# Moving the overflow branch of a mixture of experts into its last first product, in a two-layer decoder trunk

## The chip, the cores and the metric

The kernel runs as one program on one core of a Trainium2 chip (trn2). The metric is the device time of one execution in microseconds. In the text TensorE is PE (PEld its weight loads), VectorE is DVE, ScalarE is ACT, GpSimd is POOL, and SP is the engine that issues most of the DMAs.

## What is computed

Two post-norm decoder layers over 256 positions of width 2048, all in float32. Layer 0 mixes with retention and a causal convolution, layer 1 (the odd one) with sparse attention. Behind each mixer stands the same grouped top-2 mixture of 16 experts of inner width 512, and a layer norm behind each half.

```python
def reference(x, ...):
    h = x
    for layer in range(DEPTH):                       # DEPTH = 2
        m = retention_conv_mixer(h, ...) if layer % 2 == 0 else dsa_mixer(h, ...)
        h = layer_norm(DEEPNORM_ALPHA * h + m, mix_ln_g[layer], mix_ln_b[layer])
        f = grouped_moe(h, router_w, router_b, moe_w_gu[layer], moe_w_down[layer])
        h = layer_norm(DEEPNORM_ALPHA * h + f, ffn_ln_g[layer], ffn_ln_b[layer])
    return h

def grouped_moe(x, router_w, router_b, w_gu, w_down):
    ...
    for e in range(N_EXPERTS):                       # 16
        a, b = jnp.split(xt @ w_gu[e], 2, axis=-1)
        y = y + gate[:, e:e + 1] * ((jax.nn.silu(a) * b) @ w_down[e])
    return y

# dsa_mixer begins with   proj = x @ w_in            # 2048 x 4176
```

## The kernel before

Weights stream from memory in chunks of 1 MB (`w0`, `w1`, ...) into a pool of 22 pages; `pump` issues the DMA of the next chunk on SP as soon as fewer than `ringmax` chunks are held, `take` hands the next one out and `done_chunk` frees it. Chunks 240 to 255 are those of layer 0's last pair of experts, 256 on those of the odd layer's input projection.

**The experts** (`moe`) run in eight pairs i, each in two halves j, one expert at a time. An expert takes up to 64 of the positions that chose it. `gather` picks their columns by one-hot products into `X[i]`, `gu(i, j)` is the first product (8 chunks, 32 float32 matmuls that write 64 rows each, L907), `turn` transposes the activated result (`sl`) into `gT`, and `down(i, j)` is the second product (L942). `weigh` scales its result by the gate and splits it into a rounded part `Yh` (ACT, L931) and the rest `Yl` (DVE, L932), both in the type fp32r. `scatter(i, t)` puts the pair's result back in place by one-hot products of `Yh` and `Yl` (L954) and adds it on DVE to the running sum `z` (L964), for t, the two halves of the positions. It runs behind the next pair's first product.

**The last pair** is cut otherwise. Behind `gu(7, 1)` and `turn` comes `overflow`: a branch (L1070) on the largest number of positions that an expert got. Only where that exceeds 64 does its body run, a general loop over all experts; on the inputs here it is skipped. Then `last_down` (from L975) does the last second product in four column blocks b of 512 columns, one chunk each (L1005), weighs each and places it: blocks 0 and 1 by `spread`, with the sum on DVE and its statistics by `bn_stats` (L993), blocks 2 and 3 by a product of the identity with the old sum `z` that opens the accumulation in a bank (`begin`, L983, tile `psb`), onto which the placed products fall, and ACT copies the bank back (L990). `begin(2)` runs right behind the branch, `begin(3)` behind block 1. `moments` turns the statistics into mean and scale (L674 to L676, the last step on POOL).

**The odd layer** starts with `norm` (L683 to L686), which applies that mean and scale to 512 columns, and `fold(kp)`, which transposes two blocks of 128 columns (`turned`, L712, tile `psz`) and writes them as `h32` (L717, L719). `parts(kp)` splits those into `hhi` (ACT) and `hlo` (DVE). `dense` then goes through units of two such blocks: `split` rounds a half chunk into `sp` (ACT, L234) and its rest (DVE or POOL, L237), and `mm` makes three fp32r products for each block and half of the positions, hhi by sp, hhi by the rest, hlo by sp (L266 to L268): 12 a unit. A group of 512 output columns is 8 units. The hooks `("pre", i)` stand ahead of unit i. The first two units are split early, in `last_down`, with POOL for the rest.

The order on each engine is that in which the code is written; each engine goes through its own list and waits on semaphores. At the end (`final`) DVE does 16 instructions of norm, gain and bias, and SP writes the result out.

## Time and profile before

| | us |
|---|---|
| runs | 1709.57, 1707.22, 1711.1 (median 1709.57) |
| the profiled execution | 1710.37 |
| its span, first to last instruction | 1708.6 |
| PE busy in the span | 1639.9 (96%) |
| DVE, ACT, POOL busy | 743.3, 499.5, 345.4 |

A row of a timeline has the start in us from the span's start, the busy time, the engine, the line, the operation, what it writes and reads, and in brackets how long the engine was idle and what released it. A float32 matmul leaves two records (two for each product, so x4 is two products of the code), an fp32r one leaves one. Busy times of PE overlap, since matmuls are pipelined: what one costs in a row of them is the distance from start to start.

### The profile page before, as it was taken

The page shows a single profiled execution, that of the slowest core. Times are in us where ns is not written, and L with a number is a line of the kernel's source. Part 1 is how long each engine was busy: PE and PEld are TensorE (multiplying, and loading weights), DVE is VectorE, ACT ScalarE, POOL GpSimd, SP SyncE. Part 2 cuts the span into 40 slices and gives each one's busy share as a digit, 9 for nine tenths or more (in the row PEclk, how much of TensorE's full clock was granted, in tenths as well). Part 3 has the DMA queues.
Part 4 walks back from the last instruction along what each step waited for, and adds up shares of the span by engine and source line. Part 5 has one row for each costly group of instructions (what it writes and reads, how often), then busy time and mean ns, then how long its engine had stood idle before and what let it go on. Part 6 is the DMA issues. An engine that isn't in the chain of part 4 may idle for free. (4 is left out here: it accounts for less than half of the span.)

```text
span 1708.6 us, 21350 instructions
## 1 busy us (share of the span) xinstructions
PE 1639.9 (96%) x8551; PEld 1039.2 (61%) x8551; DVE 743.3 (44%) x1348; ACT 499.5 (29%) x780; POOL 345.4 (20%) x218
## 2 busy tenths in 40 slices
PE   9999999999999999999789999999999999999984
PEld 7888887786454445444268788788644445454432
DVE  5699987533123222221264675664412212232225
ACT  5434345433111111111054535553311111111101
POOL 1446664540000000000024554444000000000010
PEclk9999999999999999999989999999999999999996
DMA  9655545858999999999954554357899999999992
GB/s 341 216 196 173 172 148 192 304 197 353 376 411 421 421 421 420 422 420 420 407 186 139 171 176 145 124 200 267 319 358 416 422 420 421 421 421 420 421 413 76
DMA packets 122860, 528.29 MB, mean 309 GB/s; under 512 B 10506, under 2 KB 10898, under 8 KB 74498
## 3 DMA queue, kind: packets, MB, share of 16 engines
q1 hardware_dynamic: 122130, 525.32, 79.1%
q8 instruction: 71, 1.16, 0.3%
q0 software_dynamic: 480, 1.46, 0.2%
q14 instruction: 35, 0.29, 0.0%
q10 hardware_dynamic: 144, 0.07, 0.0%
HBM read 524.71 MB, written 2.10 MB: 308 GB/s over the span
## 5 line engine op out<-in xcount | busy, mean ns | idle before, releaser
L907 PE MATMUL pgu<-w,X 128*64 128x512 f32 x2048 | 449.8, 594 | 7.3 <-DMA w<-in_moe_w_gu_dram 7.3
L237 POOL TENSOR_TENSOR sp<-w,sp 128x1024 fp32r<-128x1024 f32 (+1 forms) x108 | 272.9, 2535 | 398.9 <-ACT sp L234 383.4
L907 PEld LDWEIGHTS pgu<-w,X 128*64 128x64 f32 x2048 | 144.0, 137 | 295.2 <-issue 267.3
L234 ACT ACTIVATE sp<-w 128x1024 fp32r<-128x1024 f32 (+1 forms) x228 | 230.4, 1045 | 121.4 <-PE acc L268 64.1
L237 DVE TENSOR_TENSOR sp<-w,sp 128x1024 fp32r<-128x1024 f32 (+1 forms) x120 | 185.3, 1547 | 129.4 <-ACT sp L234 129.1
L932 DVE SCALAR_TENSOR_TENSOR Yl<-pdn,gs,Yh 64x512 fp32r<-64x512 f32 (+1 forms) x136 | 97.7, 718 | 272.2 <-ACT Yh L931 271.2
L942 PE MATMUL pdn<-w,gT 128*64 128x512 f32 x960 | 212.6, 595 | 0.9 <-ACT gT L919 0.9
L931 ACT ACTIVATE Yh<-pdn,gs 64x512 fp32r<-64x512 f32 (+1 forms) x136 | 89.4, 657 | 306.9 <-PE pdn L942 213.0
L911 DVE TENSOR_TENSOR sl<-sl,pgu 128x256 f32<-128x256 f32 x32 | 13.5, 422 | 352.1 <-ACT sl L910 352.1
L266 PE MATMUL acc<-sp,xhi 128*128 128x512 f32 x384 | 152.2, 396 | 0.0
L267 PE MATMUL acc<-sp,xhi 128*128 128x512 f32 x384 | 149.7, 390 | 0.3 <-DVE sp L237 0.3
L268 PE MATMUL acc<-sp,xlo 128*128 128x512 f32 x384 | 149.8, 390 | 0.0
L792 POOL COPY pt<-pt 128x128 f32<-128x128 f32 x16 | 5.1, 317 | 707.1 <-DVE pt L791 707.1
L942 PEld LDWEIGHTS pdn<-w,gT 128*64 128x64 f32 x960 | 66.3, 137 | 123.4 <-issue 117.1
L910 ACT ACTIVATE sl<-pgu 128x256 f32<-128x256 f32 x32 | 12.3, 385 | 385.2 <-PE pgu L907 385.2
L470 DVE SCALAR_TENSOR_TENSOR pcv<-up,cw,pcv 128x255 f32<-128x255 f32 (+14 forms) x240 | 113.2, 472 | 7.3
L266 PE MATMUL acc<-sp,hhi 128*128 128x512 f32 x256 | 106.0, 414 | 1.2 <-ACT hhi L1125 1.2
L268 PE MATMUL acc<-sp,hlo 128*128 128x512 f32 x256 | 101.0, 395 | 1.2 <-DVE hlo L1126 1.2
L267 PE MATMUL acc<-sp,hhi 128*128 128x512 f32 x256 | 100.5, 393 | 0.0
L267 PEld LDWEIGHTS acc<-sp,xhi 128*128 128x128 f32 x384 | 72.2, 188 | 15.4 <-DVE sp L237 1.0
L268 PEld LDWEIGHTS acc<-sp,xlo 128*128 128x128 f32 x384 | 72.1, 188 | 15.3
L266 PEld LDWEIGHTS acc<-sp,xhi 128*128 128x128 f32 x384 | 72.2, 188 | 14.8 <-ACT sp L234 0.4
(305 smaller groups left out, 2067.8 us busy)
## 6 DMA issues: line engine op xcount, KB each, us to landing
w<-in_moe_w_gu_dram SPq DMA_DIRECT2D x256, 1024.0 KB, 16.5
w<-in_moe_w_down_dram SPq DMA_DIRECT2D x128, 1024.0 KB, 19.5
w<-in_even_w_in_dram SPq DMA_DIRECT2D x46, 1024.0 KB, 5.5
w<-in_odd_w_in_dram SPq DMA_DIRECT2D x32, 1024.0 KB, 5.2
w<-in_even_w_out_dram SPq DMA_DIRECT2D x16, 1024.0 KB, 8.7
w<-in_odd_w_out_dram SPq DMA_DIRECT2D x16, 1024.0 KB, 5.3
acc<-in_x_dram SPq DMA_DIRECT2D x8, 256.0 KB, 8.3
w<-in_even_w_in_dram SPq DMA_DIRECT2D x4, 512.0 KB, 6.7
```

Of the source, the lines that this page charges most:

```text
L234: nc.scalar.activation(sp[:, 0], src, AF.Copy)
L237: eng.tensor_tensor(sp[:, 1], src, sp[:, 0].bitcast(F32), ALU.subtract)
L266: nc.tensor.matmul(ac, xh[:, x], wh, start=st, stop=False)
L267: nc.tensor.matmul(ac, xh[:, x], wl, start=False, stop=False)
L268: nc.tensor.matmul(ac, xl[:, x], wh, start=False, stop=en)
L470: nc.vector.scalar_tensor_tensor(y, up[:, c, 0:S - i], w, y, op0=ALU.mult, op1=ALU.add)
L907: nc.tensor.matmul(ps[h * 64:(h + 1) * 64, :], X[i][:, k, j * 64:(j + 1) * 64], wv[:, kk, :, h, :], start=k == 0, stop=k == KT - 1)
L910: nc.scalar.activation(sl, ps[:, 0:256], AF.Silu)
L911: V.tensor_tensor(sl, sl, ps[:, 256:512], ALU.mult)
L931: nc.scalar.activation(hi, po[r, :], AF.Copy, scale=g)
L932: V.scalar_tensor_tensor(lo, po[r, :], g, hi.bitcast(F32), op0=ALU.mult, op1=ALU.subtract)
L942: nc.tensor.matmul(po[b][half * 64:(half + 1) * 64, :], gT[:, c, h * 64:(h + 1) * 64], wv[:, half ^ j, 2 * b:2 * b + 2, :], start=kk == 0, ...
```

## The change

It does five things, the same for both layers where it concerns the experts.

1. The branch and its body move from behind `turn` into `gu(7, 1)`, ahead of its chunk 3 (w247). Between `turn` and `down(7, 0)` stands a new block with a `BRANCH_PREFETCH_HINT` that names the branch as likely taken, for PE alone, and one product of ones; every engine jumps into this block and out of it. The body's buffers change (four pages, one weight tile in place of two).
2. The old sums of blocks 2 and 3 (`begin`, moved out of `last_down`) come ahead of chunks 5 and 7 of `gu(7, 1)`, so behind the branch.
3. Columns 1024 to 2047 of the last pair are weighed whole, into a float32 tile `Yw`, half by ACT and half by DVE, and placed by one float32 product where two fp32r ones stood. Behind the last of them come 12 products of ones (`warm`).
4. The odd layer's first four units (w256, w257) take `h32` and the unsplit weights, one float32 product for each three. Their early splits are gone, `norm` and `fold` are spread over the hooks, and `parts(0)` to `parts(3)` come behind unit 4.
5. `scatter(i - 1, 0)` moves ahead of chunk 4 of `gu(i, 0)` and `scatter(i - 1, 1)` ahead of `turn`; `back` lays `h` out with the even columns of each 256 ahead of the odd ones, so `gather` reads it in a row and the first `scatter` reads it in two pieces; `ringmax` is 12 in place of 8 in the last pair until the branch.

```diff
-        if self.early and eng is None:
-            u["sp"] = self.early.popleft()["sp"]
-            return
...
+        if "x32" in u:
+            u["w32"] = i, t[:, u["sub"] * w:(u["sub"] + 1) * w, :]
+            return
...
+        if "x32" in u:
+
+            i, t32 = u["w32"]
+            for kk in range(w):
+                for t in ts:
+                    nc.tensor.matmul(g.acc[t], at(u["x32"], u["k"] + kk)[:, t * P:(t + 1) * P], t32[:, kk, :], start=u["first"] and kk == 0, stop=False)
+            if u["sub"] == u["nsub"] - 1:
+                self.done_chunk(i)
+            return
...
-            o = h[t][:, c * 512:(c + 1) * 512]
+            o = h[t][:, c * 512:(c + 1) * 512].rearrange("p (q r j) -> p q r j", q=2, r=2)
+            ps = ps.rearrange("p (q j r) -> p q r j", q=2, r=2)
...
+                k = c * 4 + b
+                for t in range(2):
+                    nc.tensor.matmul(ps[:, b * P:(b + 1) * P], h[t][:, k * P:(k + 1) * P], self.PT[i][:, t, 0:P], start=t == 0, stop=t == 1)
...
             for c in range(8):
+                if also and c in also:
+                    also[c]()
...
+        whole = lambda i, c0: i == 7 and c0 >= 512
...
+            if whole(i, c0):
+                y = Y["whole"][r, o, c0 - 512:c0 - 512 + n]
+                if half:
+                    nc.scalar.activation(y, po[r, :], AF.Copy, scale=g)
+                else:
+                    V.tensor_scalar(y, po[r, :], g, None, op0=ALU.mult)
+                return
...
+            one = whole(i, c * 256)
...
-                                     start=n == 0 and not begun, stop=n == 1, skip_group_check=begun)
+                at = GT[i][0][:, o, t * P:(t + 1) * P]
+                y = [Y[i][n][:, o, c * 256:(c + 1) * 256] for n in range(2)]
+                if one:
+                    at, y = at.bitcast(F32), [Y["whole"][:, o, c * 256 - 512:c * 256 - 256]]
+                for n in range(len(y)):
+                    nc.tensor.matmul(ps[:, o * 256:(o + 1) * 256], at, y[n], start=n == 0 and not begun, stop=n == len(y) - 1, skip_group_check=begun)
...
-                V.scalar_tensor_tensor(z, h[t][:, c * 512:(c + 1) * 512], ALPHA, ps, op0=ALU.mult, op1=ALU.add)
+                for q in range(2):
+                    s = slice(q * 256, (q + 1) * 256)
+                    v = lambda x: x[:, s].rearrange("p (j r) -> p j r", r=2)
+                    V.scalar_tensor_tensor(v(z), h[t][:, c * 512:(c + 1) * 512][:, s].rearrange("p (r j) -> p j r", r=2), ALPHA, v(ps),
+                                           op0=ALU.mult, op1=ALU.add)
...
+        def last_down(gT):
...
-            begin(2, self.bank)
...
-                for half in range(2):
+                for half in (1, 0):
                     weigh(7, 1, half, po, b * 256)
-                for u in early if b == 2 else ():
-                    self.split(u, nc.gpsimd)
-                    self.early.append(u)
                 if b:
                     finish(b - 1)
-                if b == 1:
-                    begin(3, self.psum)
             finish(3)
             self.drop(2)
+            self.warm(12)
...
             if i == 7:
-                self.ringmax = 8
+                self.ringmax = 12
             if 0 < i < 7:
                 self.onehot(i + 1)
 
 
-            sl = gu(i, 0)
             if i:
-                scatter(i - 1, 0)
+                sl = gu(i, 0, {4: lambda: scatter(i - 1, 0)})
+                scatter(i - 1, 1)
                 gT = turn(sl)
-                scatter(i - 1, 1)
             else:
+                sl = gu(i, 0)
                 self.onehot(1)
                 gates(0)
                 self.ringmax = 16
                 gT = turn(sl)
+            if i == 7:
+
+                with tc.block():
+                    tc.mark_branch_hint_location(f"general{layer}", hint="LikelyTaken", engines=[mybir.EngineType.PE])
+                    self.warm(1)
             down(i, 0, gT)
...
+
+            def general():
+                self.overflow(layer, rv, h, wide)
+                self.ringmax = 8
+                if before_last:
+                    before_last()
+            sl = gu(i, 1, {3: general, 5: lambda: begin(2, self.bank), 7: lambda: begin(3, self.psum)} if i == 7 else None)
...
-        gT = turn(sl)
-        self.overflow(layer, rv, h, wide)
-        if before_last:
-            before_last()
-        last_down(gT, self.units([Group(512, None, None)])[:2] if layer == 0 else ())
+        last_down(turn(sl))
...
-        hT = [wide("ohT", S) for i in range(2)]
+        hT = [self.page(f"ohT{i}", [P, 8, S]) for i in range(2)]
         gT = self.page("ogT", [P, 8, S])
-        ow = [self.page(f"ow{i}") for i in range(2)]
+        ow = self.page("ow")
...
         def fold(kp):
-            def f():
-                self.norms(kp)
-                self.turned(kp, h32[kp // 4][:, 2 * kp % 8:2 * kp % 8 + 2, :], 64, 96)
-            return f
+            return lambda: self.turned(kp, h32[kp // 4][:, 2 * kp % 8:2 * kp % 8 + 2, :], 64, 96)
+
+        def norm(c):
+            return lambda: self.norm(c)
 
         def parts(kp):
             def f():
@@ -1338,10 +1364,19 @@
         gout = [Group(512, lambda: (oo["hi"], oo["lo"]), self.z_done(c)) for c in range(4)]
         n = 4 + 8 * 8
         hooks = {("pre", n): [start_out], ("pre", n + 12): [last_heads, close_act]}
-        hooks["pre", 0] = [fold(0), fold(1), parts(0), fold(2), parts(1)]
-        for i in range(1, 7):
-            hooks["pre", i] = ([fold(i + 2)] if i + 2 < 8 else []) + [parts(i + 1)]
-        self.dense(self.units(gin) + self.units(gout, self.oorder), lambda: self.moe_begin(1), hooks)
+        us = self.units(gin)
+
+        for u in us[:4]:
+            u["x32"] = h32
+        hooks["pre", 0] = [norm(0), fold(0), fold(1), norm(1)]
+        hooks["pre", 1] = [fold(2)]
+        hooks["pre", 2] = [fold(3), norm(2)]
+        hooks["pre", 3] = [fold(4), parts(4)]
+        hooks["pre", 4] = [fold(5), parts(5), norm(3)]
+        hooks["pre", 5] = [fold(6), parts(6), parts(0)]
+        hooks["pre", 6] = [fold(7), parts(7), parts(1)]
+        hooks["pre", 7] = [parts(2), parts(3)]
+        self.dense(us + self.units(gout, self.oorder), lambda: self.moe_begin(1), hooks)
```

On PE at the end of layer 0's last pair, before: `pgu` is the first product's bank, `pst` the transposition, `psb` the old sums, `pdn` the last second product. The skipped body is left out.

```order
L907 MATMUL pgu_5398<-w251_5386,X_5136 64x512 x4
L917 MATMUL pst_5450<-cst_69,sl_5447 128x128 x2
L1070 COMPARE_AND_BRANCH
...
L983 MATMUL psb_5739<-z0_3557,cst_69 128x512
L983 MATMUL psb_5741<-z1_3558,cst_69 128x512
L1005 MATMUL pdn_5743<-w252_5403,gT_5453 64x256 x8
L1005 MATMUL pdn_5758<-w253_5409,gT_5453 64x256 x8
```

Now the announcement stands between the transposition of the half j = 0 and its second product (w240):

```order
L921 MATMUL pst_5373<-cst_69,sl_5346 128x128 x2
L1060 UNCONDITIONAL_BRANCH
L1433 BRANCH_PREFETCH_HINT
L365 LDWEIGHTS ones_75
L365 MATMUL warm_5380<-ones_75 128x512
L1060 UNCONDITIONAL_BRANCH
L955 MATMUL pdn_5382<-w240_5185,gT_5376 64x512 x2
```

and the branch itself ahead of w247, again with the body left out:

```order
L911 MATMUL pgu_5417<-w246_5265,X_5144 64x512 x4
L1095 COMPARE_AND_BRANCH
...
L911 MATMUL pgu_5417<-w247_5271,X_5144 64x512 x4
L911 MATMUL pgu_5417<-w248_5326,X_5144 64x512 x4
L1004 MATMUL psb_5735<-z0_3530,cst_69 128x512
L1004 MATMUL psb_5737<-z1_3531,cst_69 128x512
L911 MATMUL pgu_5417<-w249_5332,X_5144 64x512 x4
L911 MATMUL pgu_5417<-w250_5338,X_5144 64x512 x4
L1004 MATMUL psb_5747<-z0_3530,cst_69 128x512
L1004 MATMUL psb_5749<-z1_3531,cst_69 128x512
L911 MATMUL pgu_5417<-w251_5344,X_5144 64x512 x4
L921 MATMUL pst_5760<-cst_69,sl_5757 128x128 x2
L1027 MATMUL pdn_5765<-w252_5388,gT_5763 64x256 x8
```

The branch and both pairs of old sums now have first products behind them, and the four blocks of the last second product follow `turn` at once.

On DVE in `last_down`, blocks 0 to 3, before (two `Yl` a block, for the two halves of the rows):

```order
L964 TENSOR_TENSOR z1_3558<-psa_5780,z1_3558 128x512
L993 BN_STATS stats_102<-z1_3558 128x6
L932 SCALAR_TENSOR_TENSOR Yl7_5389<-pdn_5791,gs_5237,Yh7_5388 64x256 x2
L964 TENSOR_TENSOR z0_3557<-psa_5814,z0_3557 128x512
L993 BN_STATS stats_102<-z0_3557 128x6
L964 TENSOR_TENSOR z1_3558<-psa_5821,z1_3558 128x512
L993 BN_STATS stats_102<-z1_3558 128x6
L932 SCALAR_TENSOR_TENSOR Yl7_5389<-pdn_5828,gs_5237,Yh7_5388 64x256 x2
L991 BN_STATS stats_102<-psb_5739 128x6
L991 BN_STATS stats_102<-psb_5741 128x6
```

and now:

```order
L987 TENSOR_TENSOR z1_3531<-psa_5802,z1_3531 128x512
L1016 BN_STATS stats_102<-z1_3531 128x6
L941 TENSOR_SCALAR Yw_5410<-pdn_5809,gs_5245 64x256
L987 TENSOR_TENSOR z0_3530<-psa_5822,z0_3530 128x512
L1016 BN_STATS stats_102<-z0_3530 128x6
L987 TENSOR_TENSOR z1_3531<-psa_5829,z1_3531 128x512
L1016 BN_STATS stats_102<-z1_3531 128x6
L941 TENSOR_SCALAR Yw_5410<-pdn_5836,gs_5245 64x256
L1014 BN_STATS stats_102<-psb_5735 128x6
L1014 BN_STATS stats_102<-psb_5737 128x6
```

For blocks 2 and 3 one scaling stands where two subtractions stood.

On PE at the odd layer's first unit, before, from the last transposition ahead of it:

```order
L712 MATMUL psz_5911<-cst_69,z0_3557 128x128
L712 MATMUL psz_5911<-cst_69,z1_3558 128x128
L712 MATMUL psz_5911<-cst_69,z0_3557 128x128
L712 MATMUL psz_5911<-cst_69,z1_3558 128x128
L266 MATMUL acc_5926<-sp_5806,hhi0_5881 128x512
L267 MATMUL acc_5926<-sp_5806,hhi0_5881 128x512
L268 MATMUL acc_5926<-sp_5806,hlo0_5883 128x512
L266 MATMUL acc_5927<-sp_5806,hhi0_5881 128x512
L267 MATMUL acc_5927<-sp_5806,hhi0_5881 128x512
L268 MATMUL acc_5927<-sp_5806,hlo0_5883 128x512
```

and now the whole of that unit:

```order
L715 MATMUL psz_5907<-cst_69,z0_3530 128x128
L715 MATMUL psz_5907<-cst_69,z1_3531 128x128
L715 MATMUL psz_5907<-cst_69,z0_3530 128x128
L715 MATMUL psz_5907<-cst_69,z1_3531 128x128
L253 MATMUL acc_5916<-w256_5422,h320_5890 128x512
L253 MATMUL acc_5917<-w256_5422,h320_5890 128x512
L253 MATMUL acc_5916<-w256_5422,h320_5890 128x512
L253 MATMUL acc_5917<-w256_5422,h320_5890 128x512
```

Four float32 products with the weight chunk itself stand where twelve with its split parts stood.

## Rows read from the trace of the kernel before

**Rows 1.** windows by stretch: us, busy of each engine, granted clock, DMA share, GB/s
```profile
540.00:840.00 300.00, 297.25 (x1606) 139.96 (x1602) 72.33 (x126) 46.14 (x79) 1.30 (x4) 1.00 1.01 421
840.00:845.00 5.00, 2.61 (x12) 0.69 (x10) 0.42 (x1) 0.77 (x2) 0.00 (x0) 1.00 1.04 385
846.00:850.00 4.00, 0.00 (x0) 0.00 (x0) 0.00 (x0) 0.00 (x0) 0.00 (x0) 0.50 1.05 381
850.00:856.00 6.00, 5.68 (x14) 2.41 (x16) 0.00 (x0) 0.00 (x0) 0.00 (x0) 0.50 1.05 386
870.00:882.00 12.00, 7.26 (x25) 5.93 (x26) 7.57 (x17) 7.08 (x13) 2.23 (x3) 0.50 0.78 250
```

**Rows 2.** timeline of TensorE, layer 0's end: start, us, [idle before <- releaser]
```profile
798.79 14.01 PE L907 MATMUL pgu<-w,X 128*64 128x512 f32 x64
...
828.34 1.94 PE L907 MATMUL pgu<-w,X 128*64 128x512 f32 x8 [0.55 <-DMA w<-in_moe_w_gu_dram]
...
840.82 1.94 PE L907 MATMUL pgu<-w,X 128*64 128x512 f32 x8 [0.58 <-DMA w<-in_moe_w_gu_dram]
843.70 0.44 PE L917 MATMUL pst<-cst,sl 128*128 128x128 f32 x2 [0.94 <-DVE sl L911]
850.32 3.75 PE L983 MATMUL psb<-z,cst 128*128 128x512 f32 x4 [6.19 <-PEq L1070]
854.00 4.67 PE L1005 MATMUL pdn<-w,gT 128*64 128x256 f32 x32
...
859.99 1.88 PE L983 MATMUL psb<-z,cst 128*128 128x512 f32 x4
861.80 1.95 PE L1005 MATMUL pdn<-w,gT 128*64 128x256 f32 x16
...
869.50 0.41 PE L954 MATMUL psb<-Yh,gtt 128*128 128x256 f32 x1 [1.58 <-ACT Yh L931]
...
879.51 0.80 PE L266 MATMUL acc<-sp,hhi 128*128 128x512 f32 x1 [1.20 <-ACT hhi L1125]
```

**Rows 3.** TensorE's waits by releaser: total us, times, longest us
```profile
PE psb L983 <- PEq L1070: 12.1, 2, 6.2
PE pgu L907 <- DMA w<-in_moe_w_gu_dram: 7.3, 14, 0.7
PE psb L954 <- ACT Yh L931: 3.2, 2, 1.6
```

**Rows 4.** timelines of TensorE and VectorE over layer 1's end
```profile
1660.75 1.94 PE L907 MATMUL pgu<-w,X 128*64 128x512 f32 x8 [0.65 <-DMA w<-in_moe_w_gu_dram]
...
1669.99 3.75 PE L983 MATMUL psb<-z,cst 128*128 128x512 f32 x4 [5.92 <-PEq L1070]
...
1691.48 0.26 DVE L674 BATCH_NORM_AGGREGATE mv<-stats 128x2 f32<-128x24 f32 x1
```

**Rows 5.** the page of the profile: its span
```profile
span 1708.6 us, 21350 instructions
```

**Rows 6.** timelines of VectorE and GpSimd over the same end of layer 0
```profile
864.29 0.48 DVE L932 SCALAR_TENSOR_TENSOR Yl<-pdn,gs,Yh 64x256 fp32r<-64x256 f32 x1 [0.80 <-ACT Yh L931]
...
865.83 0.69 DVE L964 TENSOR_TENSOR z<-psa,z 128x512 f32<-128x512 f32 x1
866.56 0.69 DVE L993 BATCH_NORM_STATS2 stats<-z 128x6 f32<-128x512 f32 x1
...
868.48 0.46 DVE L932 SCALAR_TENSOR_TENSOR Yl<-pdn,gs,Yh 64x256 fp32r<-64x256 f32 x1
...
874.06 0.54 POOL L676 TENSOR_TENSOR rs<-mv,neghalf 128x1 f32<-128x1 f32 x1 [0.55 <-DVE mv L675]
```

**Rows 7.** timeline of TensorE in the odd layer's first units
```profile
893.76 0.60 PE L712 MATMUL psz<-cst,z 128*128 128x128 f32 x4
...
896.95 0.60 PE L712 MATMUL psz<-cst,z 128*128 128x128 f32 x4
...
904.96 0.50 PE L268 MATMUL acc<-sp,hlo 128*128 128x512 f32 x1 [0.93 <-DVE hlo L1126]
```

More of the change, by code (lines that the diff above doesn't have):

```diff
@@ L87, in __init__ @@
         self.tasks = deque()
-        self.early = deque()
         self.credit = 0
@@ L235, in split @@
         self.nsplit += 1
-        eng = eng or (nc.gpsimd if self.nsplit % 2 == 0 and self.pool_split else nc.vector)
+        eng = nc.gpsimd if self.nsplit % 2 == 0 and self.pool_split else nc.vector
         eng.tensor_tensor(sp[:, 1], src, sp[:, 0].bitcast(F32), ALU.subtract)
@@ L698, in normed @@
                 nc.vector.tensor_scalar(z, z, m, rs, op0=ALU.subtract, op1=ALU.mult)
-    def norms(self, kp):
-        for c in ((0, 1), (2,), (3,))[kp] if kp < 3 else ():
-            self.norm(c)
     def turned(self, kp, out, gc, bc):
@@ L945, in down @@
                 Y[i] = [self.page(f"Y{n}{i}", [P, 2, 1024], F32R) for n in "hl"]
+                if i == 7:
+                    Y["whole"] = wide("Yw", 512)
             for b in range(2):
@@ L973, in scatter, with begin @@
                 self.drop(2)
-        def last_down(gT, early):
-            begun = {}
-            def begin(b, alloc):
-                for t in range(2):
-                    ps = begun[b, t] = alloc("psb")
-                    nc.tensor.matmul(ps, self.ident, self.acc[t][:, b * 512:(b + 1) * 512], start=True, stop=False, skip_group_check=True)
+        begun = {}
+        def begin(b, alloc):
+            for t in range(2):
+                ps = begun[b, t] = alloc("psb")
+                nc.tensor.matmul(ps, self.ident, self.acc[t][:, b * 512:(b + 1) * 512], start=True, stop=False, skip_group_check=True)
+        def last_down(gT):
             def finish(b):
```

30 lines of the change are left out of this document (13 added, 17 removed).

## The prediction

> **What bounds the kernel now.** I read the windows first, by stage. From 540 to 840 us the DMA engines are busy throughout and move 421 GB/s [rows 1]: the experts' chunks of 1 MB come every 2.49 us, whatever the engines do. TensorE is busy in 297 of these 300 us, but its busy time says little: a chunk of the first product takes 1.75 us where chunks lie ready (64 records in 14.01 us, eight a chunk), and at the end of the layer each chunk has a wait of 0.55 us ahead of it [rows 2]. So in the experts' stage the stream of weights is the bound, and moves inside it are free as long as TensorE is back in step when the last chunk of the first product lands, at 840.8 us in layer 0.
>
> What follows that landing is a bare chain, and there the time is to be had. The waits by releaser put 12.1 us on TensorE's own sequencer at the branch, in two pieces, one a layer; nothing else of TensorE's comes near, the 14 waits for expert chunks together are 7.3 [rows 3]. The timelines show it in place: the transposition ends at 844.14, then 6.19 us without anything until 850.32, and 5.92 in layer 1 [rows 2, 4]. The clock adds to that. It falls to 0.50 of 2.4 GHz (1.2 GHz) in the idle stretch and stays there until 856, and again from 870 to 882, behind a last wait of 1.58 us and the norm [rows 1, 2]. At 1.2 GHz the two old sums of block 2 take 3.7 us; the same pair at full clock, block 3's, takes 1.81 from start to start [rows 2].
>
> **The sum for layer 0,** from the profiled execution (span 1708.6 [rows 5], time 1710.37).
>
> *Branch and old sums.* The branch now comes ahead of w247, so behind w246, which is done at 830.3 [rows 2]. If the announcement works, TensorE goes on with w247 at 830.83 when it lands. From there, with 1.75 us a chunk, landings 2.49 apart and 1.81 for a pair of old sums: w247 to 832.6, w248 from 833.3 to 835.1, old sums to 836.9, w249 to 838.6, w250 to 840.4, old sums to 842.2, w251 to 844.0. Before, it was done at 842.76. So 3.6 us of old sums and the branch cost 1.2 us there, the rest lies beside the stream. Two of those sums stood in the bare chain at half clock (3.7 us), two more at full clock (1.8).
>
> *The second product.* Before, from the end of the first product to the end of blocks 0 and 1 it is 842.76 to 858.67, 15.9 us: 1.9 for activation and transposition, the branch, the old sums, and 4.67 for the two blocks, in part at half clock [rows 2]. Now it is 1.9 and twice 1.87: 5.6 us, with TensorE never idle for longer than the activation, so I take full clock. Blocks 0 and 1 end at 849.6, 9.1 us sooner. A transfer could take the place of the wait: the last four chunks come at 385 GB/s [rows 1], 2.72 us each, so they land at 843.5, 846.3, 849.0 and 851.7, and they are wanted at 845.9, 847.8, 850.8 and 854. Hidden, by 1.5 us at least.
>
> *Weighing and placing.* Now VectorE is late next. Behind block 1 it does the last two `Yl` (end 851.7, each after ACT's half), then sum and statistics of both halves for block 0 and for block 1 (8 instructions of 0.69), two scalings of at most 0.46 in place of four `Yl`, four statistics with some 0.7 of waiting for ACT's copies, and the moments, 0.54 of them on POOL [rows 6]. That ends at about 862.4; from blocks 0 and 1 12.8 us, where before it was 15.9 (858.67 to 874.60). Before, the old sums of block 3 lay in it, the early splits on ACT, and a `Yl` that stood in line until 868.48 [rows 6] and held TensorE for the 1.58 us (3.2 over both layers [rows 3]). The whole columns cost TensorE no more: a float32 product of 256 columns is half of the 0.9 of an old sum, two fp32r ones take 0.24, so four of them are 1.8 us for 0.95, beside VectorE's chain. Mean and scale are ready 12.2 us sooner.
>
> *The odd layer.* From there to the first product it was 4.9 us (879.51 [rows 2]), with norm of 1024 columns and the split of `h` in it and the transpositions at half clock. Now one norm, four transpositions and two writes stand in it: between 2.0 (first write only is waited for) and 2.7; I take 2.4, a gain of 2.5, since the 12 products of ones reach to about 862 and leave short gaps. Units 0 to 3 took 14.6 us from 879.51 to the first product of unit 4 at 894.1, the first of them at half clock. Now each is four float32 products of 0.9, no row of this shape being there but the old sum's, plus 0.36 of transpositions (893.76 to 894.12 in a unit of 3.19 [rows 7]): 15.9, a loss of 1.3. At half clock for the first two it would be 3 more. The splits put off to units 5 to 7 can hold TensorE as `hlo` did before (0.93 [rows 7]), or no longer: between 1 us lost and 1 gained, taken as nothing. Layer 0 gains 12.2 + 2.5 - 1.3 = 13.4.
>
> **Layer 1** has the same chain to its first aggregation: 1662.69 to 1691.48 [rows 4]. In layer 0's new order that point falls 17.6 us behind the old end of the first product (860.4 against 842.76), so at 1680.3: 11.2 sooner. The norm and the writes behind it stay.
>
> **What costs nothing.** The moved `scatter`, the other layout of `h` and its 16 half-size sums on VectorE lie under the stream (VectorE busy 72 of 300 us [rows 1]); were the stream not the bound, they would cost some 2 us in all. The jumps into and out of the announcing block are the unknown: no row shows an unconditional jump in mid-program. Their targets are the next instructions, so nothing should have to be fetched; the other end is a stall like the branch's. On SP, VectorE, ACT and POOL even that would be covered, SP having eight chunks under way and the others some 15 us until the activation. [...]
>
> The sum: 13.4 + 11.2 = 24.6 off 1710.37 is 1685.8; the profiled execution is 0.8 above the median of the runs, so **1685**. Its own range is 1679 to 1691, by the half clock, the units 5 to 7 and some 2 us of error in VectorE's chain.
>
> **Rival 1: the announcement does nothing.** Then the stall of 5.9 to 6.2 us comes behind w246, TensorE resumes at 836.5, and five chunks and four old sums make 12.4 us: 848.9, which is 4.9 later than above, and 3 more if the clock falls as it did before, with 6 us at 0.50 behind the stall [rows 1]. Twice that is 10 to 16: 1695 to 1701, **1697**. For it speaks that the stream can't cover a stall so near to its end; against it, that 12 us and some hundred instructions lie between announcement and branch, twice the stall. [...]
>
> **Rival 2: the jumps stall TensorE, and it ends slower.** If each of the two jumps on TensorE is itself a fetch of 6 us at the announcement, and the branch too, 18.3 us of stall and 3.6 of old sums meet 3.7 us of slack a layer (half of 7.3 [rows 3]): 18 us late, where the forecast has 1.2. That is 34 over both layers, **1719**, more with the clock. It decides from 12 us a layer, where the gain is used up. Against it: the targets are adjacent.
>
> **Rival 3: VectorE or the odd layer's start holds most of the gain back,** with the clock at 1.2 GHz through units 0 and 1 (3 us), `hlo` late (2 us) and block copies late in both layers (2 us): **1692**. For it speaks that VectorE has no slack behind block 1; against it, that its instructions there are counted and shown.
>
> **How the numbers follow.** Forecast 0.65, rival 1 0.22, rival 3 0.08, rival 2 0.03, and 0.02 for no change. A measurement of this kernel tells 0.2% (3.4 us) from nothing. The range takes in the forecast's own and rivals 1 and 3: 1679 to 1701. Faster 0.95, same 0.02, slower 0.03.
>
> **What would show it.** Right: no wait of TensorE on its sequencer over 1 us near the branch, w251's product done within 2 us of its landing plus 1.75, no granted clock of 0.50 between 844 and 862, the first product of the odd layer 14 to 15 us sooner, layer 1's first aggregation 11 sooner against the same landing. Rival 1: a 6 us wait ahead of w247. Rival 2: one ahead of w240. Wrong in another way: a later landing of the last chunk, which would say that the stream was not the bound.

## The result, and the profile after

The changed kernel takes 1686.68 us (median of 4 runs, 1684.45 to 1687.28); the kernel before, on the same chip, 1710.34 (1707.22 to 1712.38). The ratio is 0.9861, 95% interval 0.9843 to 0.9879. The forecast was 1685, by a sum of 24.6 us; the profiled execution of the changed kernel has a span of 1685.5 us for 1708.6 [rows 5], 23.1 less.

TensorE's waits by releaser (total us, times, longest us), which answer to [rows 3]:

```profile
PE pdn L955 <- ACT gT L923: 8.0, 16, 0.5
...
PE pgu L911 <- DMA w<-in_moe_w_gu_dram: 0.9, 2, 0.5
...
PE pgu L911 <- PEq L1095: 0.3, 2, 0.2
```

The 12.1 us at the branch are 0.3. The waits for expert chunks fell from 7.3 to 0.9, and in their place stand 16 waits of 0.5 for the activation that copies `gT`: `scatter(i - 1, 1)`, now ahead of `turn`, no longer covers that copy. Both lie under the stream, so one replaces the other.

The timeline of TensorE at layer 0's end, to be laid beside [rows 2]:

```profile
827.03 5.32 PE L911 MATMUL pgu<-w,X 128*64 128x512 f32 x24
832.51 1.94 PE L911 MATMUL pgu<-w,X 128*64 128x512 f32 x8 [0.16 <-PEq L1095]
834.98 1.94 PE L911 MATMUL pgu<-w,X 128*64 128x512 f32 x8 [0.53 <-DMA w<-in_moe_w_gu_dram]
836.85 1.98 PE L1004 MATMUL psb<-z,cst 128*128 128x512 f32 x4
838.76 3.65 PE L911 MATMUL pgu<-w,X 128*64 128x512 f32 x16
842.34 1.98 PE L1004 MATMUL psb<-z,cst 128*128 128x512 f32 x4
844.26 1.94 PE L911 MATMUL pgu<-w,X 128*64 128x512 f32 x8
847.13 0.44 PE L921 MATMUL pst<-cst,sl 128*128 128x128 f32 x2 [0.94 <-DVE sl L915]
848.10 3.67 PE L1027 MATMUL pdn<-w,gT 128*64 128x256 f32 x32 [0.53 <-ACT gT L923]
...
855.80 0.39 PE L974 MATMUL psa<-Yh,gtt 128*128 128x256 f32 x1 [0.24 <-DVE z L987]
...
856.47 1.95 PE L1027 MATMUL pdn<-w,gT 128*64 128x256 f32 x16
858.35 3.72 PE L974 MATMUL psb<-Yw,gtt 128*128 128x256 f32 x16
861.90 2.75 PE L365 MATMUL warm<-ones 128*128 128x512 bf16 x12
865.63 1.28 PE L715 MATMUL psz<-cst,z 128*128 128x128 f32 x8 [0.97 <-DVE z L693]
867.11 3.70 PE L253 MATMUL acc<-w,h 128*128 128x512 f32 x8 [0.20 <-DVE h L722]
...
882.62 0.48 PE L274 MATMUL acc<-sp,hhi 128*128 128x512 f32 x1
```

Row by row: the branch costs 0.16 us ahead of w247 (832.51), where it cost 6.19. The old sums (L1004) stand between the chunks. Nothing then keeps TensorE waiting longer than the 0.94 and 0.53 us around the transposition, until the placed blocks end at 862; `warm` covers part of the norm, and the odd layer's first product starts at 867.11, 12.4 us sooner than before. The first product of unit 4 is at 882.62, for 894.12. The granted clock, the column ahead of the DMA share, which showed 0.50 in two stretches here [rows 1], is 1.00 from 840 to 870; the last two windows (us, busy time of PE, PEld, DVE, ACT and POOL, clock, DMA share, GB/s):

```profile
860.00:865.00 5.00, 4.66 (x22) 2.66 (x20) 3.67 (x10) 1.90 (x4) 1.08 (x2) 1.00 0.45 128
865.00:870.00 5.00, 4.17 (x15) 2.32 (x16) 1.94 (x5) 2.53 (x4) 0.00 (x0) 1.00 1.05 397
```

In layer 1 the scale is done on POOL at 1670.8, 23.4 us sooner than before, and TensorE's timeline shows the same at the branch:

```profile
1638.23 1.94 PE L911 MATMUL pgu<-w,X 128*64 128x512 f32 x8 [0.16 <-PEq L1095]
```

Two executions of the changed kernel stand in different places, though. In the one above w248 lands late enough to start at 834.98, before the change at 833.32. In a second execution of the same kernel (the row *changed, again* below) it starts at 833.49, and the span is 1684.0, 24.6 less than before. So I compare kernels below by distances from w248's start, which leave the stream's lateness out:

| kernel | w248 starts, layer 0 | to the mean and scale | from there to unit 4 | layer 1: the same chunk to the last scale | time, median | ratio to before |
|---|---|---|---|---|---|---|
| before | 833.32 | 41.31 | 19.49 | 40.29 | 1710.34 | 1 |
| changed | 834.98 | 29.89 | 17.75 | 29.31 | 1686.68 | 0.9861 |
| changed, again | 833.49 | 29.90 | 17.75 | 29.31 | 1686.43 | 0.9853 |
| e1, no announcement | (stall) | | 17.76 | | 1696.58 | 0.9921 |
| e6, announced one chunk ahead | (stall) | | 17.76 | | 1696.14 | 0.9910 |
| e10, announced three chunks ahead | 833.86 | 29.89 | 17.76 | 29.33 | 1687.82 | 0.9871 |
| e2, before with the announcement alone | 833.49 | 32.08 | 19.26 | 31.67 | 1692.19 | 0.9899 |
| e3, branch and sums late | 835.92 | 31.37 | 17.75 | 30.80 | 1690.55 | 0.9884 |
| e7, split last columns | 835.21 | 31.41 | 17.76 | 30.94 | 1691.69 | 0.9890 |
| e8, no products of ones | 835.90 | 29.90 | 20.11 | 29.33 | 1690.58 | 0.9874 |
| e11, early splits | 833.35 | 29.84 | 19.23 | 29.31 | 1688.13 | 0.9876 |
| e4, units split late | 835.41 | 29.89 | 25.09 | 29.31 | 1693.70 | 0.9894 |
| e5, part 5 undone | 836.36 | 29.90 | 17.76 | 29.32 | 1688.15 | 0.9862 |
| e9, sums in the idle spots | 836.41 | 27.75 | 17.76 | 27.18 | 1684.15 | 0.9846 |

Start times of rows of the timelines: w248's first product, VectorE's row that makes the negative mean by scale (in layer 1 POOL's last row of the scale), the first product of unit 4. Where nothing in the chain differs the distances agree within 0.06 us, while the times move by 2 us, and the ratios have intervals of plus and minus 0.0015 to 0.002 (2.5 to 3.5 us). A difference between two changed kernels below 3 us is therefore read from the distances, not from the times. Where a row has (stall), w248 follows the stall without a wait, and its start is no measure of the stream.

### The profile page after: what moved, and what is told of

It reads as the page before. It is cut to its first block, busy times and chain, and to the rows that moved or that the text cites. A ratio compares the mean times of both kernels' runs of the same rounds, so it can differ in the third digit from the quotient of the medians.

```text
span 1685.5 us, 21370 instructions
## 1 busy us (share of the span) xinstructions
PE 1636.4 (97%) x8561; PEld 1029.7 (61%) x8561; DVE 739.5 (44%) x1357; ACT 493.4 (29%) x770; POOL 339.3 (20%) x215
## 3 DMA queue, kind: packets, MB, share of 16 engines
q0 software_dynamic: 480, 1.46, 0.2%
## 5 line engine op out<-in xcount | busy, mean ns | idle before, releaser
L236 POOL TENSOR_TENSOR sp<-w,sp 128x1024 fp32r<-128x1024 f32 (+1 forms) x105 | 265.6, 2537 | 282.0 <-ACT sp L233 256.4
L233 ACT ACTIVATE sp<-w 128x1024 fp32r<-128x1024 f32 (+1 forms) x224 | 226.4, 1045 | 120.4 <-PE acc L276 64.0
L945 DVE SCALAR_TENSOR_TENSOR Yl<-pdn,gs,Yh 64x512 fp32r<-64x512 f32 (+1 forms) x124 | 90.8, 733 | 257.0 <-ACT Yh L944 249.3
L944 ACT ACTIVATE Yh<-pdn,gs 64x512 fp32r<-64x512 f32 (+1 forms) x124 | 82.9, 669 | 249.6 <-PE pdn L955 184.0
L274 PE MATMUL acc<-sp,hhi 128*128 128x512 f32 x240 | 98.7, 411 | 0.4 <-ACT hhi L1151 0.4
L276 PE MATMUL acc<-sp,hlo 128*128 128x512 f32 x240 | 94.0, 392 | 0.0
L275 PE MATMUL acc<-sp,hhi 128*128 128x512 f32 x240 | 93.6, 390 | 0.0
```

Of the source, the lines that this page charges most:

```text
L233: nc.scalar.activation(sp[:, 0], src, AF.Copy)
L236: eng.tensor_tensor(sp[:, 1], src, sp[:, 0].bitcast(F32), ALU.subtract)
L274: nc.tensor.matmul(ac, xh[:, x], wh, start=st, stop=False)
L275: nc.tensor.matmul(ac, xh[:, x], wl, start=False, stop=False)
L276: nc.tensor.matmul(ac, xl[:, x], wh, start=False, stop=en)
L944: nc.scalar.activation(hi, po[r, :], AF.Copy, scale=g)
```

## The experiments

**The announcement, taken away (e1) and alone (e2).** e1 is the changed kernel without the block; e2 the kernel before with it.

```diff
-            if i == 7:
-                with tc.block():
-                    tc.mark_branch_hint_location(f"general{layer}", hint="LikelyTaken", engines=[mybir.EngineType.PE])
-                    self.warm(1)
             down(i, 0, gT)
```

> The changed kernel without the announcing block (no hint, no product of ones in it, no jumps); all else as in the changed kernel. Theory (the announcement does the work): TensorE stands on its sequencer for 5.9 to 6.2 us ahead of w247 in each layer, as it did at the branch before. Since TensorE is just in step with the stream there (it waited 0.53 us for w248), nearly all of it comes out behind w251: 5.5 us a layer, 11 in all, and up to 3 more a layer if the clock falls to 1.2 GHz in the stall: 1698 to 1704 us. Rival (the place alone hides the branch, the announcement is idle): no wait over 1 us ahead of w247, 1685 to 1688 us.

> The kernel before with the announcing block alone, between turn and down of expert 7,0; the branch stays behind the last transposition. Theory (the announcement alone takes the stall away wherever the branch stands): the 12.1 us on TensorE's sequencer fall below 1, the clock stays at 2.4 GHz, so layer 0's blocks 0 and 1 end near 850.5 instead of 858.67, 8 us sooner, and layer 1 gains as much: 1692 to 1696 us. Rival (a branch is cheap only under the stream): 1708 to 1712 us.

TensorE's timelines around the branch, in e1 in each layer, then in e2:

```profile
825.68 5.32 PE L911 MATMUL pgu<-w,X 128*64 128x512 f32 x24
835.12 5.35 PE L911 MATMUL pgu<-w,X 128*64 128x512 f32 x16 [4.12 <-PEq L1090]
840.40 1.99 PE L1004 MATMUL psb<-z,cst 128*128 128x512 f32 x4
```

```profile
1645.04 5.35 PE L911 MATMUL pgu<-w,X 128*64 128x512 f32 x16 [3.40 <-PEq L1090]
```

```profile
843.84 0.44 PE L917 MATMUL pst<-cst,sl 128*128 128x128 f32 x2 [0.94 <-DVE sl L911]
844.42 1.95 PE L983 MATMUL psb<-z,cst 128*128 128x512 f32 x4
```

Without the announcement the stall is back, ahead of w247, and the time rises to 1696.6 (1692.2 to 1700.6), ratio 0.9921 [0.9902, 0.9941]. It is the announcement, then, that takes the stall away, and not the place. The stall is smaller than the theory had it: 4.12 and 3.40 us, not 5.9 to 6.2, and the time lies under the theory's 1698 to 1704. The clock falls as well, for a shorter time than the theory allowed. Windows of e1 behind the stall in each layer (the granted clock ahead of the DMA share):

```profile
837.00:839.00 2.00, 2.00 (x7) 0.61 (x4) 0.00 (x0) 0.00 (x0) 0.00 (x0) 0.50 1.00 398
1646.00:1648.00 2.00, 2.00 (x6) 0.60 (x4) 0.00 (x0) 0.00 (x0) 2.00 (x2) 0.50 0.99 409
```

At 0.50, w247 and w248 take 5.28 us in each layer (835.12 to 840.40 in layer 0), where two chunks at full clock take 3.58 (838.76 to 842.34 in the changed kernel): 1.7 us a layer, not 3. Stalls and clock are 10.9 us in both layers together. Not all of it comes out, since waits for chunks fall away: from w244's start to the mean and scale it is 42.74 us in e1 and 37.84 and 37.98 in the two executions of the changed kernel, in layer 1, to the last scale, 41.44 for 37.07 and 37.05. So 9.2 to 9.3 us come out; the profiled span is 7.9 to 9.4 us longer than the two of the changed kernel.

e2 shows the other side: with the branch where it always was, the block alone takes the stall from 6.19 to less than 0.2 us and the time to 1692.2, 18.1 us less than before, of the change's 24. By the distances it is 9.23 and 0.23 in layer 0 and 8.62 in layer 1, 18.1 together. The stalls themselves are 11.8 of that; most of the rest is clock, for behind the stall two old sums take 3.68 us from start to start (850.32 to 854.00 [rows 2]), and in e2 1.89.

The two sides do not add up. All parts without the announcement (e1) bring 13.7 us, the announcement alone 18.1, both together 24: in part they save the same time. Which part of the block does it, the hint or the jumps around it, neither run tells; a block without the hint was not tried.

**How early it must be announced (e6, e10).** The block moves to one chunk and to three chunks ahead of the branch.

```diff
-gu(i, 1, {3: general, ...
+gu(i, 1, {2: announce, 3: general, ...      # e6
+gu(i, 1, {0: announce, 3: general, ...      # e10
```

> The changed kernel with the announcing block moved to one chunk ahead of the branch, ahead of w246, so that some 2 us lie between them and not 12. Theory (the announcement starts a load that takes about 6 us from then on): a stall of 3.5 to 4.2 us remains ahead of w247 in each layer, 1693 to 1697 us. Rival A (it works at once): no stall, 1685 to 1688 us. Rival B (it needs the whole of the old distance): about 6 us, as without it, 1698 to 1704 us.

> The changed kernel with the announcing block ahead of w244, three chunks (5.3 us of products) ahead of the branch, where it was one chunk with no effect and four chunks of down and three of gu with full effect. Theory (the announcement starts a load of some 6 us, and TensorE's sequencer reads it ahead of the array): most of the stall is gone, under 1.5 us a layer, 1686 to 1689 us. Rival (it takes nearly the old distance): 3.4 to 4.1 us a layer remain, 1693 to 1698 us.

The product of ones in the block (`warm`, L365) and the first row behind the branch, in e6 and in e10:

```profile
830.40 0.39 PE L365 MATMUL warm<-ones 128*128 128x512 bf16 x1
...
836.53 5.35 PE L911 MATMUL pgu<-w,X 128*64 128x512 f32 x16 [3.87 <-PEq L1095]
```

```profile
825.82 0.39 PE L365 MATMUL warm<-ones 128*128 128x512 bf16 x1
...
831.67 1.94 PE L911 MATMUL pgu<-w,X 128*64 128x512 f32 x8 [0.16 <-PEq L1095]
```

One chunk ahead the announcement gives nothing: 3.87 and 3.61 us, 7.5 together as in e1. Three chunks ahead it gives all: 0.16. The numbers of my theory for e6 came in (a stall of 3.5 to 4.2 us, and 1696.1 us in 1693 to 1697), but not as the theory meant them: it took them for the rest of a stall of 6 us, and without any announcement the stall is no more than 4.1. Rival B, about 6 us, fell. One reading fits these rows: from the block's product to the first product behind the branch it is 6.13 us in e6 (830.40 to 836.53; 5.86 in layer 1), the 5.9 to 6.2 of the stall before; in e10 5.85 us lie between them, with 0.16 of it a wait, and in the changed kernel 13. So it looks as if a load of some 6 us started when TensorE gets to the block, and in e1 as if it started some 2 us before TensorE gets to the branch. That is an argument from four rows; the last section has what bears on it. A block two chunks ahead, which should leave some 2 us, was not tried.

**The place of the branch and the old sums (e3).** Announced as in the changed kernel, but branch and sums behind the transposition.

```diff
-            sl = gu(i, 1, {3: general, 5: ..., 7: ...} if i == 7 else None)
+            sl = gu(i, 1)
...
-        last_down(turn(sl))
+        gT = turn(sl)
+        general()
+        begin(2, self.bank)
+        begin(3, self.psum)
+        last_down(gT)
```

> The changed kernel with the branch and the four old sums of each layer back behind the last transposition; the announcement stays where it is. Theory (announced, the branch costs 0.2 us anywhere, and the place matters for the 3.7 us of old sums alone): w251 is done about 1.8 us sooner, at its landing plus 1.9, and the four sums and the branch stand bare behind the transposition for 3.9 us: 2.1 us a layer lost, 1689 to 1693 us. Rival (the place under the stream hides the branch): a stall of about 6 us in each layer, 1698 us or more.

TensorE's timeline from w251 to the first second product:

```profile
843.45 1.94 PE L911 MATMUL pgu<-w,X 128*64 128x512 f32 x8 [0.61 <-DMA w<-in_moe_w_gu_dram]
846.91 3.67 PE L1004 MATMUL psb<-z,cst 128*128 128x512 f32 x8
850.51 2.81 PE L1027 MATMUL pdn<-w,gT 128*64 128x256 f32 x24
```

As the theory has it: no stall, w251 starts at its landing, and 3.6 us of old sums stand bare ahead of `pdn`. The loss is 1.48 and 1.49 us by the distances (2.1 expected: 3.2 us more between w251 and `pdn`, less the 1.75 by which w251 is earlier). Taken out of the changed kernel, the place costs 3 us of the 24 and the announcement 9 (e1); alone, the announcement gives 18 (e2).

**The last columns, split again (e7).**

```diff
-        whole = lambda i, c0: i == 7 and c0 >= 512
+        whole = lambda i, c0: False
```

> The changed kernel with the last pair's last 1024 columns split into Yh and Yl again and placed by two fp32r products. Theory (VectorE is the bound behind block 1): each of blocks 2 and 3 has two Yl of 0.49 us behind ACT's half in place of one scaling of 0.46, some 0.5 to 0.8 us more a block in VectorE's chain, so mean and scale come 1 to 1.6 us later in each layer, measured from block 0's products: 1688 to 1690 us. Rival (TensorE is the bound, two fp32r products being 0.95 us for 1.8): 0 to 1 us sooner, 1685 to 1686.5 us.

TensorE's timeline at the first placed products of block 2, the row with a wait:

```profile
861.47 0.39 PE L974 MATMUL psb<-Yl,gtt 128*128 128x256 f32 x1 [1.55 <-DVE Yl L945]
```

TensorE waits 1.55 us for a `Yl`, where before it waited as long for a `Yh` of the last blocks (3.2 in both layers [rows 3]), and mean and scale come 1.52 and 1.63 us later. The theory held: with the split columns VectorE is the bound. In the changed kernel itself the two engines run level (the second point under *Why the prediction was right*). The time is 5 us above the changed kernel's; the chain explains 3.2 of it, and in the profiled execution w248 came 1.7 us later than in the second one of the changed kernel.

**Without the products of ones (e8).** `self.warm(12)` is left out.

> The changed kernel without the twelve products of ones behind the last placed block of each layer. Theory (they hold the clock up over the norm): TensorE stands idle from 862.1 to 865.6, the granted clock falls to 0.50 behind it and the first one or two units run at 1.2 GHz, 2 to 4 us lost in layer 0, none in layer 1: 1688 to 1691 us. Rival (a gap of 3.5 us does not bring it down): clock 1.00 from 860 to 885, time within 1.5 us of the changed kernel's.

TensorE behind the placed blocks, and its granted clock there:

```profile
866.56 2.06 PE L715 MATMUL psz<-cst,z 128*128 128x128 f32 x8 [3.57 <-DVE z L693]
868.41 5.69 PE L253 MATMUL acc<-w,h 128*128 128x512 f32 x8
873.94 0.60 PE L715 MATMUL psz<-cst,z 128*128 128x128 f32 x4
```

```profile
865.00:870.00 5.00, 3.44 (x10) 2.38 (x11) 2.24 (x6) 2.14 (x4) 0.54 (x1) 0.56 1.05 400
870.00:875.00 5.00, 5.00 (x13) 2.36 (x12) 0.42 (x1) 0.51 (x1) 0.00 (x0) 0.75 1.05 387
```

3.57 us of idle time, and behind it a granted clock of 0.56 and 0.75 in these two windows, where the changed kernel has 1.00 in both: unit 0 takes 5.53 us for 3.54, the transpositions 1.85 for 1.48. Unit 4 is 2.36 us later, nothing changes in layer 1. The theory held; this is what would have been left of rival 3's clock.

**The odd layer's units (e4, e11).** Both split the first four units again; e11 has the two early splits of the kernel before as well, e4 has none.

```diff
-        for u in us[:4]:
-            u["x32"] = h32
...
-        hooks["pre", 0] = [norm(0), fold(0), fold(1), norm(1)]
+        hooks["pre", 0] = [norm(0), fold(0), parts(0), fold(1), norm(1), parts(1)]
...
+                for u in early if b == 2 else ():      # e11 alone
+                    self.split(u, nc.gpsimd)
+                    self.early.append(u)
```

> The changed kernel with the odd layer's first four units split again and each as three fp32r products (no early splits, the hooks in the changed order). Theory (part 4 pays, since a split stands ahead of the first product): the first product of the odd layer comes 1.5 to 2.5 us later, units 0 to 3 then take some 13 to 14.6 us in place of 15.5, so unit 4 starts 0 to 1.5 us later: 1686 to 1689 us. Rival (float32 products for three fp32r ones only cost, as the -1.3 us of the prediction's sum alone would have it): unit 4 starts 1 to 2.5 us sooner, 1684 to 1686 us.

> Part 4 undone in full: the changed kernel with the odd layer's first four units as three fp32r products each and with the two early splits of before, on ACT and POOL behind block 2 of the last second product; the hooks stay in the changed order. Theory (the unsplit units gain about what the prediction has, 2.5 us at the start less 1.3 in the units): ACT's two early splits of 0.97 us delay its scalings and copies by 0.5 to 1.5, hhi stands ahead of the first product for another 1.2, units 0 to 3 take 13 to 14.6 us in place of 15.5, unit 4 starts 0 to 2 us later: 1686.5 to 1689 us. Rival (the gap at the start also drops the clock to 1.2 GHz): 2 to 4 us later, 1689 to 1691 us.

TensorE's timelines at the odd layer's start, the rows with waits, in e4 and then in e11:

```profile
872.75 0.79 PE L274 MATMUL acc<-sp,hhi 128*128 128x512 f32 x1 [5.41 <-ACT sp L233]
```

```profile
866.69 0.50 PE L278 MATMUL acc<-sp,hhi 128*128 128x512 f32 x1 [1.46 <-ACT hhi L1158]
...
878.84 0.63 PE L719 MATMUL psz<-cst,z 128*128 128x128 f32 x4 [1.59 <-DVE z L697]
```

e4 fell by a cause that neither theory named: without early splits, ACT's split of the weights stands behind `hhi` in its order, and TensorE waits 5.41 us for it, with the clock at 0.50 behind. Unit 4 comes 7.3 us later, and the time is 1693.7. It prices unsplit units against splits on demand, not against the kernel before. e11 does that. Its early splits do not delay mean and scale at all (29.84), against my theory. Its first product is 3.50 us behind them for 2.24, since `hhi` is waited for (1.46). Units 0 to 3 take 15.73 for 15.51, with one wait for `norm` in it (1.59 at 878.84) and one for `hlo` (0.36); without these two it would be 13.8, in the theory's 13 to 14.6. So part 4 is worth 1.5 us here, its start alone 1.3. The wait for `norm` comes with the order of the hooks, which e11 has from the changed kernel, so this is not the price of part 4 in the order of before.

**Part 5 undone (e5).** `scatter` behind the first product and behind `turn` again, the old layout of `h` and the strided gather.

```diff
-                sl = gu(i, 0, {4: lambda: scatter(i - 1, 0)})
-                scatter(i - 1, 1)
-                gT = turn(sl)
+                sl = gu(i, 0)
+                scatter(i - 1, 0)
+                gT = turn(sl)
+                scatter(i - 1, 1)
```

> The changed kernel with part 5 undone but for the ring: the first layout of h and the strided gather, the first scatter's sums in one piece, and scatter behind the first product and behind turn as before. Theory (they lie under the stream and cost nothing): TensorE's 8 us of waits for gT go, waits for expert chunks take their place, the last chunk of layer 0's first product is done within 0.5 us of 846.2, and the time stays within 1.5 us of the changed kernel's. Rival (part 5 is what brought the last chunks 1.7 us later than before): w248 starts near 833.3 in place of 835.0, in both layers: 1682.5 to 1685 us.

TensorE's waits by releaser, the row of the expert chunks, which now heads the view:

```profile
PE pgu L911 <- DMA w<-in_moe_w_gu_dram: 3.2, 7, 0.6
```

The waits for `gT` are gone and waits for chunks have come up from 0.9 to 3.2: the exchange read above. The distances are the changed kernel's to 0.01 us. The rival falls: w248 starts at 836.36 without part 5, not near 833.3, and with it at 833.49 in the second execution. My own bound of 0.5 us on the end of w251 fell with it, by the stream's lateness, which the last section takes up.

**Towards a better kernel (e9).** Block 3's two old sums move into TensorE's two idle spots around the transposition, and the statistics of blocks 2 and 3 are written ahead of ACT's copy.

```diff
-gu(i, 1, {3: general, 5: lambda: begin(2, self.bank), 7: lambda: begin(3, self.psum)} ...
+gu(i, 1, {3: general, 5: lambda: begin(2, self.bank)} ...
...
         def turn(sl, also=None):
+            if also:
+                also(0)                  # begin(3), t = 0
             ps = self.psum("pst")
...
             nc.scalar.activation(gT, ps[:, 0:256]..., AF.Copy)
+            if also:
+                also(1)                  # begin(3), t = 1
...
-                        nc.scalar.activation(self.acc[t][:, b * 512:(b + 1) * 512], ps, AF.Copy)
                         V.bn_stats(self.stats[:, t, b, :], ps)
+                        nc.scalar.activation(self.acc[t][:, b * 512:(b + 1) * 512], ps, AF.Copy)
```

> A try at a better kernel: the changed one with the two old sums of block 3 moved from ahead of chunk 7 into TensorE's two idle spots of 0.94 and 0.53 us around the last transposition (one ahead of it, one behind), and the statistics of blocks 2 and 3 written ahead of ACT's copy of the same bank. Theory (both sit on the chain): from w248's start to mean and scale 1.2 to 2.2 us less in each layer, 1682 to 1684.5 us. Rival (the last chunk's landing holds the end of the first product, or the statistics wait for the bank anyway): under 0.7 us a layer, 1685 to 1686.5 us.

TensorE from w249 to `pdn`, and VectorE's statistics of blocks 2 and 3 (the first three of four):

```profile
840.19 5.67 PE L911 MATMUL pgu<-w,X 128*64 128x512 f32 x24
845.79 1.13 PE L1008 MATMUL psb<-z,cst 128*128 128x512 f32 x2
846.80 0.44 PE L923 MATMUL pst<-cst,sl 128*128 128x128 f32 x2
847.08 1.02 PE L1008 MATMUL psb<-z,cst 128*128 128x512 f32 x2
848.03 3.67 PE L1031 MATMUL pdn<-w,gT 128*64 128x256 f32 x32
```

```profile
859.72 1.28 DVE L1017 BATCH_NORM_STATS2 stats<-psb 128x6 f32<-128x512 f32 x2
861.17 0.70 DVE L1017 BATCH_NORM_STATS2 stats<-psb 128x6 f32<-128x512 f32 x1 [0.16 <-PE psb L978]
```

The two sums (L1008) fill the gaps, and `pdn` starts 11.62 us behind w248 for 13.12. VectorE's statistics no longer stand behind ACT's copies. (They are still one behind the other, though both only read the bank: ACT's copy at 861.90 is released by the statistics, after 0.27 us. What the move changes is which of the two the chain waits for.) The chain is 2.15 us shorter in layer 0 and 2.13 in layer 1. The time is 1684.15 (five runs, 1681.83 to 1685.49), ratio 0.9846 [0.9829, 0.9864]. Against the changed kernel's 0.9853 [0.9837, 0.9870] the times alone do not settle it; the distances say 4.3 us, and the profiled execution had its stream 1.4 to 2.9 us later than those of the changed kernel.

## Why the prediction was right

The direction, the size and the mechanism held, 1686.7 for 1685, but for one wait (the second point). Point by point, by the distances:

- *Branch and old sums.* Right in kind. From w248's start to the end of w251 it took 11.22 us (834.98 to 846.20) for 10.7: a pair of old sums is 1.91 to 1.92 from start to start, not 1.81, a chunk 1.79, not 1.75, and the last chunk's end is 1.94 behind its start.
- *Second product, weighing and placing.* From w251's end to mean and scale 18.67 us (846.20 to 864.87), for 18.4. The length is right, but the wait behind it is not: VectorE is not alone in being "late next", TensorE takes as long. From the second product on (848.10) TensorE shows one idle time up to the last placed product, the 0.24 us at 855.80. At the end its float32 products come at some 0.89 us a bank (four banks from 858.35 to 861.90), ACT's copies wait for them, and VectorE's statistics for the copies:

```profile
859.51 0.60 ACT L1013 ACTIVATE z<-psb 128x512 f32<-128x512 f32 x1 [0.58 <-PE psb L974]
```

```profile
860.14 0.70 DVE L1014 BATCH_NORM_STATS2 stats<-psb 128x6 f32<-128x512 f32 x1 [0.27 <-ACT z L1013]
```

So the 1.8 us of float32 products for 0.95, put "beside VectorE's chain" at no cost, fill the slack there was. That the sum of VectorE's instructions and 0.7 us of waiting came out to 0.3 us although TensorE sets the pace at the end is in part luck. e7 lengthens VectorE's work by two short `Yl` for one scaling a block, and then it is the bound, by 1.5 us.
- *The odd layer.* 2.24 us to the first product for 2.4, and 15.51 for units 0 to 3 for 15.9. Counted from w248, that product comes 14.1 us sooner, as the sign had it (14 to 15); as the rows stand it is 12.4, with the stream late. The guess that a float32 product of this shape costs what an old sum does was good: 0.89 (four in 867.11 to 870.65, eight records).
- *Layer 0 in all:* 11.42 + 1.74 = 13.16 us for 13.4. *Layer 1:* 10.98 for 11.2. Together 24.1 for 24.6. The span of the first profiled execution is 23.1 less, since its w248 came 1.66 us later than before, from unit 4 to the same chunk of layer 1 it took 1.2 less (757.89 for 759.05), and the end behind the last scale took 0.5 more. In the second execution w248 came only 0.17 later; that its span is 24.6 less, the forecast's sum to the tenth, is luck.
- *Rival 1.* Its condition did not hold, but e1 builds it, and 1696.6 lies on its 1697. The number came by terms of other sizes: the stall is 7.5 us in both layers together where I had about 12, the clock costs 1.7 a layer where I had 3, and 9.2 to 9.3 us come out along the chain where I had 10 to 16. Unannounced, the branch stalled TensorE in e1 (4.12 and 3.40 us) and in the kernel before (6.19 and 5.92); announced 13 us ahead it cost 0.16, which decides against the rival.
- *Rival 2.* The jumps into and out of the block cost nothing to be seen: in e6, where they stand between two chunks, the rows run on without an idle time in brackets (830.40, behind a row that ends at 830.46).
- *Rival 3.* The granted clock stayed at 1.00 from 860 to 885 us, by the products of ones (without them 0.56 and 0.75, and unit 4 comes 2.36 us later, e8).
- *The clock.* The traces give it as a share of full speed; where the prediction and the expectations write a frequency, 1.00 or 0.50 is what was measured. In the kernel before fp32r products of 512 columns came 0.43 us apart at 0.50 (880.53 to 882.66, five of them) and 0.23 at 1.00 (888.05 to 890.32, ten), 1.2 and 2.3 columns a ns.
- *What was mis-sized:* the slack under the stream. I had 3.7 us a layer left; what is left by the waits is 0.5 a layer. TensorE is now just in step with the stream at w247, which is why most of what e1 loses there comes out.

## What to carry over

A taken branch that stalls an engine in a bare chain is worth an announcement ahead of anything else: here it gave 18 us of 24 by itself; three chunks, 5.7 us, ahead of the branch were enough, and one chunk, 2.3 us, gave nothing. Then fill the short idle spots that are left in the chain (0.9 and 0.5 us around a transposition held an old sum each), and hold the clock with idle products where the next stage starts behind a norm (2.36 us in e8). Compare variants by distances between rows of one chain, since the starting point of a stage moves from execution to execution (w248 by 1.5 us, 834.98 and 833.49) as much as some of these changes bring (1.5 us in e3 and in e7).

## What I had not expected of the hardware

The stream's lateness goes with TensorE's clock ahead of layer 0's experts, and it differs between executions of one kernel. The window from 390 to 400 us (the same columns as above) in the kernel before, the first execution of the changed kernel, and its second:

```profile
390.00:400.00 10.00, 7.22 (x96) 5.55 (x96) 6.63 (x22) 5.24 (x12) 0.54 (x1) 1.00 1.01 422
```

```profile
390.00:400.00 10.00, 7.25 (x85) 5.59 (x83) 6.03 (x16) 4.53 (x10) 0.54 (x1) 0.83 1.01 423
```

```profile
390.00:400.00 10.00, 7.22 (x96) 5.55 (x96) 6.62 (x22) 5.24 (x12) 0.55 (x1) 1.00 1.01 424
```

The granted clock is 1.00, 0.83 and 1.00 from 390 to 400 us, in a stretch where TensorE is busy 7.2 of 10 us, and the experts' first product then starts at 407.60, 409.04 and 407.41. In e9 it was 0.83 there and 0.94 from 280 to 300 as well, and 410.17. The late starts are the executions whose w248 comes late, 400 us on (834.98 and 836.41, for 833.32 and 833.49). All fourteen profiled executions agree: in the six with 1.00 in both windows (280 to 300, 390 to 400) the first product starts at 407.4 to 407.8, in the eight with less in one or both at 408.9 to 410.2. So nearly the same work gets the full clock in some executions and not in others, and 1.4 to 2.8 us go with it. That the clock is the cause is read from this agreement; no run changes it there.

The other one is the stall itself: 6.19 and 5.92 us behind a transposition for which TensorE had waited (0.94 us), 4.12 and 3.40 where the branch stands between products that lie ready. The trace also has DMA packets of the kind *instruction* (71 on queue q8 and 35 on q14 in the kernel before). Those of 16 KB on queue q8 I take for TensorE's, by where they fall: in the kernel before, in e1 and in e6 one falls into each of the six stalls. It starts 3.30 and 3.24 us into the stall before, 1.44 and 0.73 in e1, 1.16 and 0.93 in e6; it takes 1.06 to 1.25 us; and TensorE goes on 1.58 to 1.64 us behind its landing in all six. So the stalls differ in the time up to the packet alone. What sets that time no run shows, nor whether TensorE's sequencer comes to branch and block ahead of the array, as the theory of e10 has it.

The same packets limit the reading of e6 and e10. In e10 one starts 2.93 us behind the block's product (1.41 in layer 1) and lands ahead of the branch. In the changed kernel there is only the one at 823.92 between block and branch, which has its like in e1, without announcement, at 822.50; and it has 69 such packets in all, where e1, e6 and e10 have 71. So announced early, the branch costs no packet of its own, and a load that starts at the block is not the whole of it.
